# A fused transformer block: another order of filler products, the inverse's rows loaded behind their stores, evictions ahead, and ten operations on another engine

## The chip, the cores and the metric

The kernel runs on one core of a Trainium2 chip. The time is that of the device for one execution, in microseconds; the profile shows one such execution with its five engines: TensorE (PE), VectorE (DVE), ScalarE (ACT), GpSimd (POOL) and the sync engine (SP), which issues the transfers.

## The reference

One transformer block on a sequence of 1024 tokens of width 1024, batch 1, in float32:

```python
mod = silu(c) @ w_ada + b_ada                  # shifts, scales, gates
h = rmsnorm(x) * (1 + sc1) + sh1
q_a, k_a, v_a, q_d, k_d, v_d, z_d, b_d, a_d = split(h @ w_in)
y_attn  = dilated_attention(q_a, k_a, v_a)     # 8 heads of 64, 3 branches
y_delta = gated_deltanet(q_d, k_d, v_d, z_d)   # 8 heads of 64
x = x + g1 * (concat(y_attn, y_delta) @ w_out)
h = rmsnorm(x) * (1 + sc2) + sh2
x = x + g2 * ((silu(h @ w_gate) * (h @ w_up)) @ w_down)   # d_ff 2816
return rmsnorm(x)
```

In the delta part, q, k and v pass a causal convolution of width 4 and a silu. The sequence is cut into chunks of 64. Each chunk and head needs the solution of a unit lower triangular 64x64 system built from k, its decays and beta, and then a scan over the chunks carries a 64x64 state. The output is normalised per head, multiplied by the gain `delta_norm_g` of 64 numbers and by silu(z).

## The kernel before

Every large product is made in three parts, with a high and a low half of both operands (names ending in h and l: `hh`, `hl`, `wh_...`, `wl_...`; the loaded weight is `wr_...`). ScalarE makes the high half, another engine subtracts to get the low half.

**Groups and filler.** The delta heads are worked in two groups of four, `delta(0)` and `delta(1)`. Their chains are long and narrow, so TensorE is given other products between their steps: the generator `others()` yields projections in small pieces, and `turn(...)` emits some of them before each step. The projections are those of the second group (kd, qd, vd by `group1`; each of them is spilled to memory for later), the gates z0 and z1 of both groups (`proj_t` with `z_evac`), and the attention's values va0, va1 and its keys and queries a4_*, a0_* (`proj_d` with `spill`). `until(...)` runs the filler up to a named projection and `hold(what, us)` runs it up to one and then some microseconds more, as the plan counts them; `LEVELS` gives the two arguments for each group. The modulation's later columns (`mods`, from loads `wm` of 512 KB) come in bursts inside the filler, unless `quiet[0]` is set.

**Evictions.** A finished filler product sits in one of two PSUM banks. ScalarE copies it to a buffer of a ring of four (tag `ev`): zt by a Silu (line 634), va (line 1087), sp_* (line 1096). The sync engine stores the buffer. POOL multiplies zt by the gain before the store (line 635).

**The inverse.** `delta_prep` makes lt, the off-diagonal parts, and stores it (line 813). `delta_v` convolves v and multiplies by beta (vd, trv, vb). `delta_inverse` loads lt back as rows (nt, line 870), multiplies them (line 875) and solves 32x32 blocks in 31 pairs of VectorE operations (tm, tt; lines 886 and 890). The result goes to memory and back as tn (lines 893 and 895). Four heads then build the 64x64 and 128x128 inverses: the first product lv (line 918) needs tn, as do ScalarE's copies to `t64`, named tc (lines 924 and 925), and VectorE's transposes to U (line 923). The heads start `SKEW` steps apart, and no modulation is emitted while they run. `delta_scan` follows.

**After the scan** the rest of the filler runs inside the attention, and y is loaded with its halves (`y_load`, line 1403 on), multiplied by w_out and normalised.

**The feed-forward part** uses sums of operands to save products, in two levels. x2[k, half] is the normalised input. At its start, t2[k], T1, T2, T3, T4, H11, H21 and H22 are such sums or single tiles, each split by `h2_split(name, k, tile, engine)`: ScalarE makes the high half (line 1472), the engine named makes the low half by a subtraction (line 1473). `sub` is a difference (line 1596). The products of gate (wga, wgb, wgc) and up (wua, ...) take them in the order H11, H21, then for the last weights T2, T1, T3, H22, T4.

Within an engine the order is that of the priorities that the code gives while it is emitted; an instruction waits for all that stands ahead of it on its engine.

## Time and profile before

| | |
|---|---|
| median of 3 runs | 1410.61 us (1410.28 to 1413.69) |
| the profiled execution | 1409.24 us, its span 1407.2 us |
| mean granted TensorE clock | 0.993 |
| TensorE busy | 1347.5 us, 96% of the span |
| VectorE, ScalarE, POOL busy | 875.2, 661.7, 285.8 us |
| modulation loads (wm) | 44 of 512 KB, 6.2 us to landing |

A row of a timeline is: start in us, duration, engine, line and operation, output <- input, shape, and in brackets the idle time before it with what ended it. A row of the windows gives the stretch, its length, the busy time of PE, PEld, DVE, ACT and POOL with instruction counts, the granted clock, the share of the DMA engines and GB/s. A row of waits gives the total in us, how often, and the longest. A row of grouped instructions gives busy time and the mean in ns. The time outside the span is 2.0 us.

### The profile page before, as it was taken

Reading aid. Unit: us, or ns where it says so; the run is one execution under the profiler, and the core shown is the slowest. Engines: PE = TensorE matmul, PEld = TensorE weight load, DVE = VectorE, ACT = ScalarE, POOL = GpSimd, SP = SyncE. Lnnn points to the kernel's source line nnn. Section 1 sums busy time; section 2 is a strip of 40 time slices with the busy share of each in tenths; the row PEclk is TensorE's granted clock in tenths of the full one; section 3 lists DMA queues with packets and bytes.
Section 4 is the critical chain, followed back from the end, with each engine's and each line's share of the span. In section 5 each row is a group of like instructions: output and inputs, shape, how many; then the busy total and the mean of one; then the engine's idle time right before and its main releaser. Section 6 shows DMA issues by size and latency. Waiting matters only on the chain.

```text
span 1407.2 us, 24465 instructions
## 1 busy us (share of the span) xinstructions
PE 1347.5 (96%) x8984; PEld 1109.5 (79%) x8984; DVE 875.2 (62%) x1669; ACT 661.7 (47%) x1287; POOL 285.8 (20%) x267
## 2 busy tenths in 40 slices
PE   8999999998989899999989999999999999999997
PEld 4778877888878677777877878888888888888885
DVE  3687484656815533666227986667585776474487
ACT  4497514356224355766147743333333333444456
POOL 2345412444303344453153000000000000000000
PEclk9999999999999999999999999999999999999999
DMA  8665575486352345621485345545363665765566
GB/s 307 224 194 167 153 214 164 134 255 186 109 143 65 125 138 145 195 97 61 160 247 175 130 158 171 173 148 174 131 206 105 213 211 185 253 224 194 195 225 232
DMA packets 169872, 245.68 MB, mean 175 GB/s; under 512 B 32566, under 2 KB 73831, under 8 KB 169752
## 3 DMA queue, kind: packets, MB, share of 16 engines
q1 hardware_dynamic: 169752, 244.12, 53.5%
q8 instruction: 71, 1.16, 0.3%
q14 instruction: 49, 0.40, 0.1%
HBM read 181.30 MB, written 67.48 MB: 177 GB/s over the span
## 4 chain that ended last, share of the span: by engine, by line
PE 58%; DVE 3%; DMA 2%; issue 1%; ACT 1%; POOL 0%; SPq 0%; DVEq 0%; ACTq 0%; POOLq 0%
PE wua L1590 8%; PE wga L1590 8%; PE X L1785 6%; PE wo L590 5%; PE wgc L1590 4%; PE wuc L1590 4%; PE Z L1785 4%; PE g_a L590 3%; PE y L1348 3%; PE wgb L1590 2%; PE Y L1785 2%; PE wub L1590 2%; PE tr L1331 2%; PE S L1307 1%; PE S L1308 1%
## 5 line engine op out<-in xcount | busy, mean ns | idle before, releaser
L1580 DVE TENSOR_TENSOR wl_db<-wr_db,wh_db 128x512 fp32r<-128x512 f32 x77 | 53.2, 691 | 76.2 <-ACT wh_db L1579 75.9
L1579 ACT CAST wh_db<-wr_db 128x512 fp32r<-128x512 f32 x77 | 47.9, 622 | 98.4 <-PE X L1785 41.3
L1311 DVE CUSTOM_DVE_ANT_0 X<-S,ng 128x512 f32<-128x512 f32 (+3 forms) x64 | 36.9, 586 | 56.2 <-PE S L1308 37.8
L1785 PE MATMUL X<-wl_db,wh_da 128*128 128x512 f32 x176 | 68.6, 390 | 0.2 <-DVE wl_db L1580 0.2
L1785 PE MATMUL X<-wh_db,wh_da 128*128 128x512 f32 x176 | 68.6, 390 | 0.0
L1785 PE MATMUL X<-wh_db,wl_da 128*128 128x512 f32 x176 | 68.5, 389 | 0.0
L1316 ACT ACTIVATE X<-X,sc 128x128 f32<-128x128 f32 (+7 forms) x64 | 49.4, 773 | 38.3 <-DVE sc L1311 34.8
L1318 POOL TENSOR_SCALAR X<-X,sc 128x128 f32<-128x128 f32 (+7 forms) x64 | 50.5, 792 | 75.9 <-DVE sc L1317 72.6
L1580 DVE TENSOR_TENSOR wl_da<-wr_da,wh_da 128x512 fp32r<-128x512 f32 x77 | 52.7, 685 | 1.2 <-ACT wh_da L1579 1.2
L590 PE MATMUL g_a<-hh,wh_a 128*128 128x512 f32 x128 | 52.8, 412 | 0.0
L590 PE MATMUL wo<-yh,wh_wo 128*128 128x512 f32 x128 | 51.3, 403 | 0.8 <-DVE xo L1399 0.8
L590 PE MATMUL wo<-yl,wh_wo 128*128 128x512 f32 x128 | 50.4, 393 | 1.1 <-DVE yl L1410 1.1
L590 PE MATMUL g_a<-hh,wl_a 128*128 128x512 f32 x128 | 51.2, 400 | 0.0
L590 PE MATMUL g_a<-hl,wh_a 128*128 128x512 f32 x128 | 51.1, 399 | 0.0
L590 PE MATMUL wo<-yh,wl_wo 128*128 128x512 f32 x128 | 51.0, 398 | 0.0
L1579 ACT CAST wh_da<-wr_da 128x512 fp32r<-128x512 f32 x77 | 47.3, 616 | 5.9 <-PE wua L1590 5.8
L1331 PE MATMUL tr<-ident,X 128*128 128x128 f32 x288 | 44.0, 277 | 3.6 <-DVE et L1334 2.0
L1579 ACT CAST wh_wg_s<-wg_s 128x512 fp32r<-128x512 f32 x33 | 20.6, 623 | 56.1 <-PE wuc L1590 23.8
L231 POOL TENSOR_TENSOR wl_wo<-wr_wo,wh_wo 128x512 fp32r<-128x512 f32 x24 | 32.9, 1374 | 61.6 <-ACT wh_wo L230 61.6
L613 PE MATMUL g_va<-wh_va,hh 128*128 128x256 f32 x128 | 38.6, 301 | 5.8 <-ACT sp_a L1096 5.8
L1331 PEld LDWEIGHTS tr<-ident,X 128*128 128x128 f32 x288 | 33.2, 140 | 13.3 <-issue 4.3
L1348 PE MATMUL y<-et,va 128*64 128x128 f32 x576 | 43.2, 280 | 0.3 <-DVE yl L1360 0.3
(544 smaller groups left out, 4304.3 us busy)
## 6 DMA issues: line engine op xcount, KB each, us to landing
wm<-in_wada SPq DMA_DIRECT2D x44, 512.0 KB, 6.2
wr_da<-ao_d SPq DMA_DIRECT2D x77, 256.0 KB, 3.0
wr_wu<-in_wu SPq DMA_DIRECT2D x50, 256.0 KB, 2.8
wr_wg<-in_wg SPq DMA_DIRECT2D x48, 256.0 KB, 2.8
ao_d<-a SPq DMA_DIRECT2D x44, 256.0 KB, 2.3
wr_wd<-in_wdn SPq DMA_DIRECT2D x44, 256.0 KB, 3.0
wr_db<-wt_d SPq DMA_DIRECT2D x44, 256.0 KB, 2.8
ao_d<-as SPq DMA_DIRECT2D x33, 256.0 KB, 2.0
```

The source lines that it names most:

```text
L231: (eng or nc.gpsimd).tensor_tensor(out=lo[:, :n], in0=raw[:, :n], in1=hi[:, :n].bitcast(F32), op=ALU.subtract)
L590: last[0] = nc.tensor.matmul(ps, a[:, w0], b[k0 + k4][:, cs], start=(i == 0), stop=(i == n - 1))
L613: last[0] = nc.tensor.matmul(ps[:, :n], a[k][:, ts_], b[:, w0], start=(i == 0), stop=(i == 23))
L1311: nc.vector.tensor_tensor_reduce(out=X[:, c0:c1], in0=ps[:, 0 : c1 - c0], in1=ng[:, u + c0 : u + c1], scale=1.0, scalar=(3e38 if m is None ...
L1316: nc.scalar.activation(X[:, 0:nk], X[:, 0:nk], AF.Exp, scale=-1.0, bias=m, accum_out=sc[:, 2:3])
L1318: nc.gpsimd.tensor_scalar(out=X[:, 0:nk], in0=X[:, 0:nk], scalar1=sc[:, 3:4], scalar2=0.0, op0=ALU.mult, op1=ALU.add)
L1331: nc.tensor.transpose(ps[:, (kb - c0) * P : (kb - c0 + 1) * P], X[:, kb * P : kb * P + P], ident)
L1348: nc.tensor.matmul(yps[64 * e : 64 * e + 64, yc], va[:, kb, 64 * e : 64 * e + 64], ets[e][:, kb, :], start=(kb == 0), stop=(kb == qb),)
L1579: nc.scalar.copy(hi, src)
L1580: (eng or nc.vector).tensor_tensor(out=lo, in0=src, in1=hi.bitcast(F32), op=ALU.subtract)
L1590: nc.tensor.matmul(ps, a[:, w0], b, start=(first and k == 0 and n_ == 0), stop=(k == 3 and n_ == 2), skip_group_check=True,)
L1785: nc.tensor.matmul(bank[b], a[:, ts_], w, start=(first and f == 0 and n_ == 0), stop=(f == NF - 1 and n_ == 2), skip_group_check=True,)
```

## The change

1. The filler's order. Before: z0, then kd, qd, vd of the second group, z1, then va0, a4_0, a0_0, va1 and so on. After: kd, qd, z0, vd, va0, z1, a4_0, a0_0, va1 and so on. `LEVELS` names z0 instead of qd for the first group's heads, and 24 us instead of 46 for the second's; the first group's scan waits for z0 instead of qd.
2. nt and bpr are loaded by a new `delta_rows_in`, right behind the stores of lt and ahead of `delta_v`. From the second group's last v on, eviction stores and modulation loads are emitted behind that load (`held`), and no modulation is emitted from there to the end of the heads. The modulation's products are tied behind the last filler product emitted.
3. ScalarE's copies tc from tn are tied behind the last eviction emitted before the heads (`evicted`).
4. The gain leaves zt and is applied where y is loaded, as a column of 128 numbers (`ngc`): a multiplying ScalarE copy and a scalar_tensor_tensor on VectorE.
5. In the feed-forward part, the low halves of H22 (four), the differences x2[4+k, 0] - t2[k] (four) and the low halves of T4 for k = 0 and 1 move from VectorE to POOL.

```diff
 EARLY = 1
-LEVELS = ("qd", 4), ("z1", 46)
+LEVELS = ("z0", 4), ("z1", 24)
 TAIL = 4
...
     dtb = small("dtb", [P, 8], I["dtb"].to_broadcast([P, 8]))
-    ngh = small("ngh", [P, 64], I["ng"].to_broadcast([P, 64]))
+    ngc = small("ngc", [P, 1], I["ng"])
 
...
     kd, qd = {}, {}
-    last = [None]
+    last, taken = [None], [None]
     fill = [None]
...
             with urgent():
-                nc.scalar.activation(zt, ps[:, 0:256], AF.Silu)
-            nc.gpsimd.tensor_tensor(
-                out=zt.rearrange("p (h d) -> p h d", h=4),
-                in0=zt.rearrange("p (h d) -> p h d", h=4),
-                in1=ngh.unsqueeze(1).to_broadcast([P, 4, 64]), op=ALU.mult,
-            )
-            nc.sync.dma_start(_.zg[TB * g + tb], zt)
+                taken[0] = nc.scalar.activation(zt, ps[:, 0:256], AF.Silu)
+            with held():
+                nc.sync.dma_start(_.zg[TB * g + tb], zt)
         return f
...
 
-    def delta_v(g, st, vps):
+    gate = [None]
+
+    def held():
+
+        return tc.issue_after(gate[0].ins) if gate[0] else ExitStack()
+
+    def delta_rows_in(g, st):
+
+        nt = pr.tile([P, 32, 32], F32, name=f"nt{g}", tag="dt", bufs=2)
+        rows = nc.sync.dma_start(nt.rearrange("p j i -> p (j i)"), _.lt[g])
+        bpr = pd.tile([P, 32], F32, name=f"bpr{g}", tag="nbpT", bufs=1)
+        nc.sync.dma_start(
+            bpr, bass.AP(tensor=_.bp[g].tensor, offset=_.bp[g][0:1, :].offset, ap=[[32, P], [1, 32]])
+        )
+        st["nt"] = nt, bpr
+        return rows
+
+    def delta_v(g, st, vps, rows):
         st["vb"] = []
...
             conv(8 + hp, vps[q](), vd)
+            if g == q == 1:
+                gate[0], quiet[0] = rows, True
             vb = pd.tile([P, 8, P], F32, name=f"vb{hp}", tag="vb", bufs=2)
...
 
-        nt = pr.tile([P, 32, 32], F32, name=f"nt{g}", tag="dt", bufs=2)
-        nc.sync.dma_start(nt.rearrange("p j i -> p (j i)"), _.lt[g])
-        bpr = pd.tile([P, 32], F32, name=f"bpr{g}", tag="nbpT", bufs=1)
-        nc.sync.dma_start(
-            bpr, bass.AP(tensor=_.bp[g].tensor, offset=_.bp[g][0:1, :].offset, ap=[[32, P], [1, 32]])
-        )
+        nt, bpr = st["nt"]
         nc.vector.tensor_tensor(
...
                 nc.vector.transpose(U[bs, :, bs], tnh[bs])
-            nc.scalar.copy(t64[0:32, :, 0:32], tnh[0:32])
-            nc.scalar.copy(t64[32:64, :, 32:64], tnh[32:64])
+            with tc.issue_after(evicted.ins):
+                nc.scalar.copy(t64[0:32, :, 0:32], tnh[0:32])
+                nc.scalar.copy(t64[32:64, :, 32:64], tnh[32:64])
             yield
...
                     hold(*LEVELS[g])
-                    front, quiet[0] = last[0].ins, True
+                    front, evicted, quiet[0] = last[0].ins, taken[0], True
                 heads.append(head(step // SKEW))
...
             with urgent():
-                nc.scalar.copy(t, ps[:, 0:256])
-            nc.sync.dma_start(_.va[c][:, :, tb].rearrange("i p d -> p i d"), t.rearrange("p (i d) -> p i d", i=2))
+                taken[0] = nc.scalar.copy(t, ps[:, 0:256])
+            with held():
+                nc.sync.dma_start(_.va[c][:, :, tb].rearrange("i p d -> p i d"), t.rearrange("p (i d) -> p i d", i=2))
         return f
...
                 with urgent():
-                    nc.scalar.copy(t, ps[:, 256 * i : 256 * i + 256])
-                nc.sync.dma_start(dst[:, HALF * hf + 256 * i : HALF * hf + 256 * i + 256], t)
+                    taken[0] = nc.scalar.copy(t, ps[:, 256 * i : 256 * i + 256])
+                with held():
+                    nc.sync.dma_start(dst[:, HALF * hf + 256 * i : HALF * hf + 256 * i + 256], t)
         return f
...
                 t0 = 16 + 4 * i
-                with urgent(), tc.issue_after(last[0].ins if i + k0 > 0 else loads[0].ins):
+                with urgent(), tc.issue_after(last[0].ins if i + k0 > 0 else loads[0].ins), held():
                     nc.sync.dma_start(
...
             for k, w in enumerate(ws_, k0):
-                rows4(ps, cc[:, k : k + 32], w, 4, k == KT - 1, k == 0)
+                with tc.issue_after(last[0].ins) if last[0] else ExitStack():
+                    rows4(ps, cc[:, k : k + 32], w, 4, k == KT - 1, k == 0)
             ws_ = after
...
 
+        yield from group1(("kd", "qd"))
         yield from proj_t(I["wz0"], 256, "z0", z_evac(0))
-        yield from group1(("kd", "qd", "vd"))
-        yield from proj_t(I["wz1"], 256, "z1", z_evac(1))
-        done.add("z1")
+        done.add("z0")
+        yield from group1(("vd",))
         for hp in range(4):
...
                 done.add(f"va{hp}")
+            if hp == 0:
+                yield from proj_t(I["wz1"], 256, "z1", z_evac(1))
+                done.add("z1")
             for col, kk in ((KA, 4), (QA, 0)):
...
         delta_prep(g, st, norms[g], kt[0:2], delta_rows(g))
+        rows = delta_rows_in(g, st)
         if g == 1:
             until(lambda: "vd" in done)
-        delta_v(g, st, [lambda q=q: vxp[q] if g == 0 else fetch(4 + q, f"v{2 + q}") for q in range(2)])
+        delta_v(g, st, [lambda q=q: vxp[q] if g == 0 else fetch(4 + q, f"v{2 + q}") for q in range(2)], rows)
         delta_inverse(g, st)
-        until(lambda: ("qd", "z1")[g] in done)
+        until(lambda: ("z0", "z1")[g] in done)
         delta_scan(g, st)
...
 
-    def y_load(k, src):
+    def y_load(k, src, gain=None):
         for hf in range(2):
...
             nc.sync.dma_start(r, src[:, cs])
-            nc.scalar.copy(yh[k][:, cs], r)
-            nc.vector.tensor_tensor(out=yl[k][:, cs], in0=r, in1=yh[k][:, cs].bitcast(F32), op=ALU.subtract)
+            if gain is None:
+                nc.scalar.copy(yh[k][:, cs], r)
+                nc.vector.tensor_tensor(out=yl[k][:, cs], in0=r, in1=yh[k][:, cs].bitcast(F32), op=ALU.subtract)
+            else:
+                nc.scalar.mul(yh[k][:, cs], r, gain)
+                nc.vector.scalar_tensor_tensor(
+                    out=yl[k][:, cs], in0=r, scalar=gain, in1=yh[k][:, cs].bitcast(F32), op0=ALU.mult, op1=ALU.subtract
+                )
 
...
         for k in range(4, 8):
-            y_load(k, _.yd[k // 2 - 2][k % 2])
+            y_load(k, _.yd[k // 2 - 2][k % 2], ngc)
         fill[0] = out_delta()
...
     for k in range(4):
-        h2_split("H22", k, x2[4 + k, 1], nc.vector)
+        h2_split("H22", k, x2[4 + k, 1], nc.gpsimd)
     for k in range(4):
-        sub(x2[4 + k, 0], x2[4 + k, 0], t2[k])
-        h2_split("T4", k, x2[4 + k, 0], nc.vector)
+        sub(x2[4 + k, 0], x2[4 + k, 0], t2[k], nc.gpsimd)
+        h2_split("T4", k, x2[4 + k, 0], nc.gpsimd if k < 2 else nc.vector)
     sx.close()
...
         "dtb": ct(A["dt_bias"]),
-        "ng": ct(A["delta_norm_g"]),
+        "ng": ct(np.tile(A["delta_norm_g"].reshape(64), 2).reshape(P, 1)),
         "wfirst": ct(first.reshape(KT, P, 512)),
```

The sync queue around the load of the second group's rows, before (nt1 and bpr1 are the rows, lt1_d their stored parts, zt and va eviction buffers, wm modulation loads):

```order
L813 DMA lt1_d_1094<-dt1_3_3559 32x8x32
L1119 DMA wm_7_0_4376<-in_wada 128x2x512
L1119 DMA wm_7_2_4378<-in_wada 128x2x512
L813 DMA lt1_d_1094<-dt1_3_3559 32x8x32 x3
L640 DMA zg15_d_1089<-zt1_7_4055 128x256
L1088 DMA va0_d_1072<-va0_0_4108 128x2x128
L1088 DMA va0_d_1072<-va0_1_4137 128x2x128
L1088 DMA va0_d_1072<-va0_2_4186 128x2x128
L870 DMA nt1_4226<-lt1_d_1094 128x1024
L872 DMA bpr1_4228<-bp1_d_1092 128x32
```

and after:

```order
L229 DMA wr_a0_0_0_4488<-in_wd 128x512
L229 DMA wr_a0_0_1_4494<-in_wd 128x512
L809 DMA lt1_d_1094<-dt1_2_3546 32x8x32 x3
L809 DMA lt1_d_1094<-dt1_3_3551 32x8x32 x4
L850 DMA nt1_3828<-lt1_d_1094 128x1024
L1132 DMA wm_6_4_5075<-in_wada 128x2x512
L1132 DMA wm_6_6_5077<-in_wada 128x2x512
L1100 DMA va0_d_1072<-va0_7_4051 128x2x128
L636 DMA zg8_d_1082<-zt1_0_4104 128x256
L636 DMA zg9_d_1083<-zt1_1_4132 128x256
```

The load nt1 follows the last store of lt1_d directly; zg8 to zg10 and the wm_6 loads stand behind it.

ScalarE around the heads' first copies in the second group, before (sp_a0_0_1 and va1_0 are evictions, tc copies from tn1, wh casts of weights):

```order
L1096 COPY sp_a0_0_0_1_4626<-g_a0_0_0_4598 128x256
L230 CAST wh_va1_3_4680<-wr_va1_3_4679 128x512
L924 COPY tc_1_0_4851<-tn1_4328 32x8x32
L925 COPY tc_1_0_4851<-tn1_4328 32x8x32
L230 CAST wh_a4_1_0_5615<-wr_a4_1_0_5614 128x512
L1096 COPY sp_a0_0_1_0_4655<-g_a0_0_1_4629 128x256
L1096 COPY sp_a0_0_1_1_4658<-g_a0_0_1_4629 128x256
L924 COPY tc_1_1_4917<-tn1_4328 32x8x32
L925 COPY tc_1_1_4917<-tn1_4328 32x8x32
L924 COPY tc_1_2_4994<-tn1_4328 32x8x32
L925 COPY tc_1_2_4994<-tn1_4328 32x8x32
```

and after:

```order
L1108 COPY sp_a0_0_0_0_4525<-g_a0_0_0_4500 128x256
L1108 COPY sp_a0_0_0_1_4528<-g_a0_0_0_4500 128x256
L230 CAST wh_va1_3_4581<-wr_va1_3_4580 128x512
L230 CAST wh_a4_1_0_5611<-wr_a4_1_0_5610 128x512
L1108 COPY sp_a0_0_1_0_4556<-g_a0_0_1_4531 128x256
L1108 COPY sp_a0_0_1_1_4559<-g_a0_0_1_4531 128x256
L1098 COPY va1_0_4611<-g_va1_0_4586 128x256
L935 COPY tc_1_0_4631<-tn1_4297 32x8x32
L936 COPY tc_1_0_4631<-tn1_4297 32x8x32
L935 COPY tc_1_1_4697<-tn1_4297 32x8x32
L936 COPY tc_1_1_4697<-tn1_4297 32x8x32
```

Both halves of sp_a0_0_1 and the first va1 stand ahead of tc_1_0 now, and so does the cast of wh_a4_1_0.

VectorE where the feed-forward part's last sums are made, before:

```order
L1473 TENSOR_TENSOR H22l0_8719<-x2_4_1_8147,H22h0_8718 128x512
L1473 TENSOR_TENSOR H22l1_8721<-x2_5_1_8148,H22h1_8720 128x512
L1473 TENSOR_TENSOR T3l3_8749<-x2_3_1_8146,T3h3_8748 128x512
L1473 TENSOR_TENSOR H22l2_8723<-x2_6_1_8149,H22h2_8722 128x512
L1473 TENSOR_TENSOR H22l3_8725<-x2_7_1_8150,H22h3_8724 128x512
L1596 TENSOR_TENSOR x2_4_0_8151<-x2_4_0_8151,t2_0_9039 128x512
L1596 TENSOR_TENSOR x2_5_0_8152<-x2_5_0_8152,t2_1_9048 128x512
L1596 TENSOR_TENSOR x2_6_0_8153<-x2_6_0_8153,t2_2_9057 128x512
L1473 TENSOR_TENSOR T4l0_8751<-x2_4_0_8151,T4h0_8750 128x512
L1599 TENSOR_TENSOR wg0_u5_9149<-wga0_8758,wg0_u5_9149 128x512
L1473 TENSOR_TENSOR T4l1_8753<-x2_5_0_8152,T4h1_8752 128x512
L1473 TENSOR_TENSOR T4l2_8755<-x2_6_0_8153,T4h2_8754 128x512
```

after:

```order
L1497 TENSOR_TENSOR T3l2_8731<-x2_2_1_8129,T3h2_8730 128x512
L1620 TENSOR_TENSOR x2_3_1_8130<-x2_7_1_8134,x2_3_1_8130 128x512
L1497 TENSOR_TENSOR T4l2_8739<-x2_6_0_8137,T4h2_8738 128x512
L1497 TENSOR_TENSOR T4l3_8741<-x2_7_0_8138,T4h3_8740 128x512
L1497 TENSOR_TENSOR T3l3_8733<-x2_3_1_8130,T3h3_8732 128x512
L1708 TENSOR_TENSOR a11_0_9191<-p1_wg0_8756,p1_wu0_8822 128x512
```

and on POOL after, at the end of its program, where nothing stood before:

```order
L1620 TENSOR_TENSOR x2_4_0_8135<-x2_4_0_8135,t2_0_9023 128x512
L1620 TENSOR_TENSOR x2_5_0_8136<-x2_5_0_8136,t2_1_9032 128x512
L1620 TENSOR_TENSOR x2_6_0_8137<-x2_6_0_8137,t2_2_9041 128x512
L1497 TENSOR_TENSOR H22l0_8703<-x2_4_1_8131,H22h0_8702 128x512
L1497 TENSOR_TENSOR H22l1_8705<-x2_5_1_8132,H22h1_8704 128x512
L1497 TENSOR_TENSOR H22l2_8707<-x2_6_1_8133,H22h2_8706 128x512
L1497 TENSOR_TENSOR H22l3_8709<-x2_7_1_8134,H22h3_8708 128x512
L1620 TENSOR_TENSOR x2_7_0_8138<-x2_7_0_8138,t2_3_9050 128x512
L1497 TENSOR_TENSOR T4l0_8735<-x2_4_0_8135,T4h0_8734 128x512
L1497 TENSOR_TENSOR T4l1_8737<-x2_5_0_8136,T4h1_8736 128x512
```

Ten operations have moved; T4l2, T4l3 stay on VectorE, now ahead of T3l3, and read what POOL writes.

## The prediction

> **What bounds the kernel now.** I read the page first (busy time, chain), then the waits of TensorE, then the windows to place them, then the engines' timelines around the longest one.
>
> ```profile
> PE 1347.5 (96%) x8984; PEld 1109.5 (79%) x8984; DVE 875.2 (62%) x1669; ACT 661.7 (47%) x1287; POOL 285.8 (20%) x267
> PE 58%; DVE 3%; DMA 2%; issue 1%; ACT 1%; POOL 0%; SPq 0%; DVEq 0%; ACTq 0%; POOLq 0%
> ...
> PE g_va L613 <- ACT sp_a L1096: 5.8, 1, 5.8
> PE trv L857 <- ACT vd L557: 4.5, 3, 2.4
> PE wua L1590 <- ACT wh_wu_s L1579: 1.2, 1, 1.2
> ```
>
> TensorE is busy 1347.5 of 1407.2 us and carries the chain. The change takes no product away and adds none, so it can only move the 60 us in which TensorE is idle, or that lie in a lower clock. The first wait line is the largest that touches the edited code.
>
> ```profile
> 389.02 0.28 PE L613 MATMUL g_va<-wl_va,hh 128*128 128x256 f32 x1
> 395.06 0.58 PE L613 MATMUL g_va<-wh_va,hh 128*128 128x256 f32 x1 [5.77 <-ACT sp_a L1096]
> 395.44 0.41 PE L613 MATMUL g_va<-wh_va,hl 128*128 128x256 f32 x1
> ...
> 400.78 0.29 PE L613 MATMUL g_va<-wl_va,hh 128*128 128x256 f32 x1
> 400.90 0.28 PE L613 MATMUL g_va<-wh_va,hh 128*128 128x256 f32 x1
> ...
> 390.00:400.00 10.00, 4.94 (x23) 4.94 (x24) 1.74 (x4) 3.84 (x10) 1.27 (x1) 0.70 0.79 206
> ```
>
> The matmul at 400.78 is the 27th after the one at 389.02. At the step of 0.12 us between the last two rows of matmuls it would have started at 389.02 + 27 x 0.12 = 392.26. It is 8.5 us late: 5.8 us of waiting, the rest because the granted clock falls (0.70 over the window) and a matmul takes 0.41 instead of 0.28 us.
>
> **Why it waits.** ScalarE stands in front of a copy of tn, the inverse's rows, which is not there yet. The evictions sp_a that would free a PSUM bank stand behind it in ScalarE's order.
>
> ```profile
> 393.00 0.40 ACT L924 COPY tc<-tn 32x256 f32<-32x256 f32 x1 [8.82 <-DMA tn<-tn_d]
> 394.37 0.64 ACT L1096 COPY sp_a<-g_a 128x256 f32<-128x256 f32 x2
> ...
> 385.85 0.32 SPq L893 DMA_DIRECT2D tn_d<-tt  x1
> 388.53 0.37 SPq L895 DMA_DIRECT2D tn<-tn_d  x1
> ...
> 351.82 0.69 DVE L860 TENSOR_TENSOR vb<-trv,beta 128x512 f32<-128x512 f32 x1 [1.90 <-PE trv L857]
> 353.03 1.22 DVE L875 TENSOR_TENSOR nt<-nt,bpr 128x1024 f32<-128x1024 f32 x1
> 355.15 0.31 DVE L218 STREAM_TRANSPOSE t<-tri 128x128 f32<-128x128 f32 x1 [0.91 <-ACT tri L1137]
> 355.38 0.15 DVE L886 TENSOR_TENSOR tm<-nt,tt 128x31 f32<-128x31 f32 x1
> 385.63 0.19 DVE L890 TENSOR_TENSOR tt<-tt,tm 128x31 f32<-128x31 f32 x1
> 393.08 1.79 DVE L923 STREAM_TRANSPOSE U<-tn 32x256 f32<-32x256 f32 x4 [7.25 <-DMA tn<-tn_d]
> ...
> 412.16 1.20 PE L918 MATMUL lv<-tn,dt 32*32 32x32 f32 x64
> ```
>
> So tn's path is VectorE's 30 us of tm and tt steps, then 7.2 us from the end of the last one to the landing (385.82 to 393.00). TensorE reaches lv, the first product that needs tn, at 412.16, long after tn. What hurts is the ScalarE order, not tn itself.
>
> **The change, part by part.**
>
> *Evictions ahead of the copies.* The hole as it stands goes: -8.5 us.
>
> *Fewer products ahead of lv.* In the new order 231 instead of 336 va matmuls stand ahead of the first lv, and the four bursts of the modulation that stood there are behind it. At 0.12 us, and at 1.08 us for a burst (below), that is 12.6 + 4.3 us. They are not saved, they come behind. But TensorE now reaches lv at 412.16 - 8.5 - 12.6 - 4.3 = 386.8, and tn must be there.
>
> ```profile
> 353.70 1.08 PE L211 MATMUL mods<-wm,cc 128*32 128x128 f32 x32
> ...
> 342.87 3.74 SPq L1088 DMA_DIRECT2D va_d<-va  x3
> 346.80 0.34 SPq L870 DMA_DIRECT2D nt<-lt_d  x1
> ...
> 312.68 1.28 ACT L634 ACT_TABLE_LOAD   x1
> 317.05 1.28 ACT L771 ACT_TABLE_LOAD   x1
> 341.23 1.28 ACT L557 ACT_TABLE_LOAD   x1 [2.98 <-DVE vd L553]
> ```
>
> *tn earlier.* The rows' load nt no longer stands behind three stores of va on the sync queue, and the nt multiply moves ahead of the last vb, into the 1.90 us in which VectorE waited there. That is 1.2 us, the 0.9 us wait for tri goes with the modulation, and the two transposes and sums of the modulation inside the chain give about 0.6. tn then lands at 393.0 - 2.7 = 390.3, the late bound. Early bound: the second z's Silu no longer falls among the decays, so the loads at 312.68 and 317.05 go, and the one at 341.23 is done by a z eviction before vd needs it. If all three (3.8 us) are on tn's path, it lands at 386.5. TensorE is there at 386.8, less the 1.3 us of its own table wait below, so it waits between 1.0 and 4.8 us. The second step of the heads needs the U transposes (1.79 us), which before were done long ahead: up to 0.9 us more. With the lost clock, which cost 2.7 us in the old hole, the price is 1 to 8.4. I take 2.5, nearer the low end, since TensorE and tn gain from the same table loads.
>
> *Table loads on the path.* TensorE's 2.4 us wait for vd held one load: -1.3 us, bounds -2.4 (the whole wait) and 0 (it is back as a wait for the conv).
>
> *Held stores and loads.* The stores of four eviction buffers and the loads wm queue behind nt's load; nt's load waits for its own stores. The wm loads of the last modulation come late, and their matmuls stand in TensorE's order inside the heads:
>
> ```profile
> wm<-in_wada SPq DMA_DIRECT2D x44, 512.0 KB, 6.2
> ```
>
> From the order I estimate about 5 us of products (some 40 at 0.12 us) between their issue and their use, so a wait of some 1 us, bounds 0 and 3. I take +0.5, because the fill around it is also what the wait covers.
>
> *Gain folded into y's load.* 16 multiplies less on POOL, and eight scalar_tensor_tensor in place of eight subtractions on VectorE: 0. Cover: TensorE's products of wo, which waited 1.1 us for yl once; without cover, eight times the difference of 0.07 us between the 0.75 and the 0.68 us of such operations in the rows below.
>
> *Ten operations from VectorE to POOL, before the gate and up products of the second half.* This part speaks against the change.
>
> ```profile
> 744.88 1.78 DVE L1473 TENSOR_TENSOR H11l<-x,H11h 128x512 fp32r<-128x512 f32 x1
> 748.29 0.68 DVE L1473 TENSOR_TENSOR H11l<-x,H11h 128x512 fp32r<-128x512 f32 x1
> 748.89 1.41 DVE L1503 SCALAR_TENSOR_TENSOR x<-x,G,rs 128x512 f32<-128x512 f32 x2
> 753.95 3.18 DVE L1503 SCALAR_TENSOR_TENSOR x<-x,G,rs 128x512 f32<-128x512 f32 x2
> 783.18 0.75 DVE L1503 SCALAR_TENSOR_TENSOR x<-x,G,rs 128x512 f32<-128x512 f32 x1
> ...
> 711.36 1.29 POOL L231 TENSOR_TENSOR wl_wo<-wr_wo,wh_wo 128x512 fp32r<-128x512 f32 x1 [1.43 <-ACT wh_wo L230]
> 753.58 3.00 POOL L1541 TENSOR_TENSOR acc<-acc,sq 128x512 f32<-128x512 f32 x2 [5.76 <-ACT sq L1540]
> ...
> 805.51 1.89 DVE L1596 TENSOR_TENSOR x<-x,t 128x512 f32<-128x512 f32 x3
> 814.46 0.50 PE L1590 MATMUL wua<-T2h,wh_wu_s 128*128 128x512 f32 x1 [1.24 <-ACT wh_wu_s L1579]
> 815.62 0.50 PE L1590 MATMUL wua<-T2h,wl_wu_s 128*128 128x512 f32 x1 [0.42 <-DVE wl_wu_s L1580]
> ...
> 790.00:800.00 10.00, 10.00 (x46) 8.29 (x45) 10.00 (x17) 6.80 (x13) 0.00 (x0) 1.00 0.18 65
> ```
>
> VectorE is fully busy in that stretch (10.00 of 10.00), and TensorE follows it closely: it waits 1.24 and 0.42 us right after. Ten operations at the 0.60 us that three of them take apart (1.89 for three) are 6.0 us less for VectorE. But while POOL works, VectorE's operations with two inputs in SBUF stand still: two of them took 3.18 us beside two on POOL (3.00 us) and 1.41 us without, so each POOL operation cost VectorE 0.9 us. Ten cost 9, and VectorE ends 3 us later than before instead of 6 earlier. Bounds: -1.7 if POOL's work falls into gaps (the two waits go), and 9.0 us less slack at the top, from POOL's own 1.5 us apiece in that row (15.0 - 6.0). Of the 3 us, half is absorbed where products stand ready ahead of need. I take +1.5. Nothing else covers it: without the slack it is 3.
>
> A rule speaks to this. The Trainium skill, "SBUF — State Buffer", section "Who interferes with whom", says that a VectorE instruction with two SBUF inputs contends with a GpSimd one that reads SBUF, and that the port pair is an exclusive lock on which the loser blocks entirely. The rows agree that VectorE is held (3.18 against 1.41 us), by less than POOL's whole duration. By the rule in full, ten times 1.29 us are lost, and this term would be 12.9 - 6.0 = 6.9 instead of 1.5.
>
> *Left over.* The 16.9 us of products that come behind lv go into the scan and the attention stage, where TensorE has short waits; 0, with -1.5 as the best case if they fill some, and +1 if evictions collide there.
>
> **The sum.** -8.5 + 2.5 - 1.3 + 0.5 + 1.5 = -5.3 us. The profiled execution took 1409.24 us (span 1407.2 and 2.0 around it), so it would take 1403.9. The median of the three runs shown, 1410.61, is 1.4 above that execution, so the median after is 1405.3.
>
> **Rivals.** About 0.3%, 4.2 us, is what a measurement of this kernel can tell from no change: faster is below 1406.4, slower above 1414.8.
>
> 1. *The hole closes and POOL hides its work.* lv waits 1.0 at its early bound, POOL falls into gaps (-1.7): -8.5 + 1.0 - 1.3 + 0.5 - 1.7 = -10.0, 1400.6. For it: tn and TensorE arrive within about 1 us of each other by the early bound. Against: VectorE has no gap between 790 and 800.
> 2. *The hole moves to lv.* tn is at its late bound, TensorE waits 5.7 us there and loses 2.4 to the clock, 5.6 more than the sum has: +0.3, 1410.9, no change. For it: tn's path is 30 us of VectorE steps that the change does not shorten. This is also the rival that the change does not do what it says.
> 3. *POOL holds VectorE for its whole length.* Place: the T2, T1, T3, H22 and T4 products at 799 to 813. At 15.0 us for ten, VectorE is 9.0 us late; if the waits of TensorE there are long enough to lower the clock as at 395, 2.7 more. The sum is -5.3 - 1.5 + 11.7 = +4.9, 1415.5, slower. It decides above 11.0 us lost there. For it: VectorE is saturated and two T4 lo operations that stay on it now wait for POOL by way of ScalarE. Against: 0.9 us per operation measured. With 1.29 us apiece, the duration of a POOL operation alone (12.9 - 6.0 = 6.9 us), it is -5.3 - 1.5 + 6.9 = +0.1, 1410.7, no change: that is what the Trainium skill's rule above gives.
>
> **Chances.** The forecast 45%, rival 1 12%, rival 2 18%, rival 3 in the form that ends slower 12%, in its mild form 8%, anything else 5%, split 3 to 2. Part of the forecast's own spread (7 of its 45) lies above 1406.4. That gives faster 0.53, same 0.33, slower 0.14. The range 1398 to 1413 reaches from below rival 1 over rival 2 and the mild rival 3, and leaves out the slower end.
>
> **What would show it.** Right: the wait of g_va for sp_a is gone from TensorE's waits; the granted clock of that stretch is 1.00; lv starts near 388 with a wait of 1 to 3 us; ACT_TABLE_LOAD is two fewer. The VectorE rows between 780 and 815 stretch to 1.4 us or more wherever a POOL row runs, and TensorE's waits at T2, T3 or T4 total 2 to 4 us. Wrong: a wait over 4 us at lv with a low clock (rival 2), T products that wait over 6 us (rival 3), or a wait for zt or sp_a evictions behind the held stores, which none of the terms holds at more than 0.5.

## The result, and the profile after

| | before | after |
|---|---|---|
| median | 1410.72 us (20 runs, 1405.68 to 1415.06) | 1405.52 us (20 runs, 1400.93 to 1411.42) |
| ratio of the two | | 0.9966, interval 0.9955 to 0.9978 |
| the profiled execution, its span | 1409.24, 1407.2 us | 1407.41, 1405.6 us |
| mean granted TensorE clock | 0.993 | 0.991 |

The forecast was 1405.3 us, and the kernel took 1405.52. The total came out within 0.3 us although several of its terms were far off. The profiled execution of after lies 1.9 us above its median and that of before 1.5 us below, so the spans differ by 1.6 us where the medians differ by 5.2.

The page of the changed kernel, busy times and chain:

```profile
PE 1353.3 (96%) x8984; PEld 1113.2 (79%) x8984; DVE 874.6 (62%) x1659; ACT 660.0 (47%) x1285; POOL 287.2 (20%) x261
PE 71%; DVE 13%; DMA 6%; ACT 4%; issue 3%; POOL 1%; SPq 0%; DVEq 0%; ACTq 0%; POOLq 0%
```

TensorE has as many instructions as before (8984) and is busy 5.8 us longer: some matmuls became slower. The waits of TensorE in the changed kernel:

```profile
PE g_z L613 <- POOL wl_z L231: 3.1, 1, 3.1
PE wga L1614 <- ACT wg_u L1670: 2.2, 1, 2.2
PE yt L1075 <- DVE o L1065: 2.2, 4, 1.4
...
PE g_z L613 <- ACT zt L634: 1.9, 1, 1.9
...
PE wga L1614 <- DVE T2l L1497: 1.8, 1, 1.8
PE x2t L1476 <- DVE x L1553: 1.6, 2, 1.0
...
PE wua L1614 <- DVE wl_wu_s L1604: 0.9, 1, 0.9
...
PE st L1009 <- DVE R L1000: 0.7, 1, 0.7
...
PE lv L928 <- DMA tn<-tn_d: 0.7, 1, 0.7
...
PE wgc L1614 <- DVE p_wg L1623: 0.5, 1, 0.5
```

The wait of g_va for sp_a is gone, and lv waits only 0.7 us. New are a wait of g_z for a weight's low half (3.1 us) and one for zt (1.9 us). At the start of the feed-forward part the waits (wg_u, T2l, wl_wu_s, p_wg) come to 5.4 us; the kernel before had 1.2 and 0.4 there.

The same profile around lv, the timelines of TensorE and VectorE:

```profile
393.40 1.20 PE L928 MATMUL lv<-tn,dt 32*32 32x32 f32 x64 [0.67 <-DMA tn<-tn_d]
...
355.70 0.18 DVE L896 TENSOR_TENSOR tm<-nt,tt 128x31 f32<-128x31 f32 x1
384.67 0.19 DVE L900 TENSOR_TENSOR tt<-tt,tm 128x31 f32<-128x31 f32 x1
393.45 1.78 DVE L933 STREAM_TRANSPOSE U<-tn 32x256 f32<-32x256 f32 x4 [8.59 <-DMA tn<-tn_d]
```

The chain of tm and tt starts no earlier than before (355.70 against 355.38), ends 1.0 us earlier (384.86 against 385.82), and its way through memory takes 8.6 us instead of 7.2. So tn lands at 393.4, not between 386.5 and 390.3. TensorE, forecast at lv for 386.8, comes there at 392.7, and the two meet.

What made both late stands 55 us earlier in the same profile, in the timelines of POOL, TensorE and ScalarE and in a window:

```profile
332.42 5.74 POOL L836 TENSOR_TENSOR qd<-qd,eb 128x1024 f32<-128x1024 f32 x2 [7.09 <-ACT eb L835]
338.10 2.25 POOL L231 TENSOR_TENSOR wl_z<-wr_z,wh_z 128x512 fp32r<-128x512 f32 x1
...
337.03 0.28 PE L613 MATMUL g_z<-wh_z,hl 128*128 128x256 f32 x1
340.41 0.58 PE L613 MATMUL g_z<-wl_z,hh 128*128 128x256 f32 x1 [3.10 <-POOL wl_z L231]
340.79 0.41 PE L613 MATMUL g_z<-wh_z,hh 128*128 128x256 f32 x1
...
346.34 1.04 PE L872 MATMUL trv<-ident,vd 128*128 128x128 f32 x8
...
341.95 1.05 ACT L557 ACTIVATE vd<-vd 128x1024 f32<-128x1024 f32 x1
...
340.00:350.00 10.00, 9.59 (x60) 9.59 (x61) 4.02 (x5) 2.86 (x4) 3.63 (x4) 0.70 0.37 92
```

The transposes trv in the kernel before:

```profile
343.64 1.09 PE L857 MATMUL trv<-ident,vd 128*128 128x128 f32 x8 [2.36 <-ACT vd L557]
```

The new order of the filler puts z1 where va0's products ran before. The low half of its last slab stands on POOL behind the two long multiplications of qd, and TensorE waits 3.1 us for it. The granted clock then falls to 0.70 for the ten microseconds from 340, in which a matmul takes 0.41 instead of 0.28 us. The transposes trv stand behind these products in TensorE's order. Their input, the Silu of vd, is done at 343.0, but they start at 346.34, without a wait of their own; before, they started at 343.64, as soon as the Silu was done. So vb and then the chain of tm and tt come later than the prediction had them.

**Where the time went, by stages.** Four points in each trace: the end of the last kk_k (the second group's products before the inverse), the start of the first lv of the second group, the start of the x2t product that waits for xt (the last transposes before the feed-forward part), and the end. Times in us of one execution each, so that differences of a few tenths mean nothing:

| | to kk_k | kk_k to lv | lv to x2t | x2t to the end | TensorE idle, lv to x2t |
|---|---|---|---|---|---|
| before | 334.0 | 78.1 | 340.8 | 654.2 | 19.0 |
| after | 333.4 | 60.0 | 349.2 | 663.0 | 10.6 |

By the prediction's count, 16.9 us of products went behind lv, and TensorE's busy time in the stage lv to x2t grew by as much (321.85 to 338.63 us, first row before, second after):

```profile
412.16:752.96 340.80, 321.85 (x2469) 259.68 (x2468) 171.23 (x470) 173.16 (x377) 138.02 (x133) 1.00 0.43 133
393.40:742.64 349.24, 338.63 (x2701) 278.05 (x2701) 170.87 (x478) 178.58 (x390) 136.92 (x133) 1.00 0.48 146
```

The stage grew by only 8.4 us: its idle time fell by 8.4. Before, these waits stood there (1.9 of the 3.2 us of yt lie in the first group's scan, outside this stage):

```profile
PE yt L1064 <- DVE o L1054: 3.2, 7, 1.2
...
PE x2t L1452 <- DVE x L1529: 2.7, 2, 1.6
PE tr L1331 <- DVE et L1334: 2.0, 3, 0.7
PE st L998 <- DVE R L989: 1.9, 1, 1.9
...
PE S L1307 <- DVE sc L1311: 1.6, 3, 1.2
```

After, yt has no wait left in this stage, x2t and st wait 1.6 and 0.7 us, and tr and S wait 0.7 us each for et and sc. Two traces do not say which part of the change did that; the amount of filler is tried below.

The last stage grew by 8.8 us. There are two causes. One is the ten operations on POOL; the timelines of POOL, VectorE and TensorE in the changed kernel, and the clock:

```profile
778.49 4.78 POOL L1497 TENSOR_TENSOR H22l<-x,H22h 128x512 fp32r<-128x512 f32 x3 [2.76 <-ACT H22h L1496]
...
780.32 1.79 DVE L1497 TENSOR_TENSOR T2l<-t,T2h 128x512 fp32r<-128x512 f32 x1
792.35 0.68 DVE L1497 TENSOR_TENSOR T2l<-t,T2h 128x512 fp32r<-128x512 f32 x1
...
793.09 0.50 PE L1614 MATMUL wga<-T2l,wh_wg_s 128*128 128x512 f32 x1 [1.75 <-DVE T2l L1497]
799.55 0.50 PE L1614 MATMUL wga<-T3h,wh_wg_s 128*128 128x512 f32 x1 [2.24 <-ACT wg_u L1670]
...
800.00:810.00 10.00, 10.00 (x38) 7.70 (x36) 7.34 (x13) 3.41 (x6) 0.00 (x0) 0.83 0.70 235
```

An operation of VectorE takes 1.79 us beside one of POOL and 0.68 us otherwise. The other cause was not foreseen. The matmuls that use the tiles H11 and H21 became slower, all through the part; durations as smallest, median and largest in ns, first before, then after:

```profile
L1590 PE MATMUL wua<-H11h,wh_wu x44: 389/389/475, 772.1 to 1170.9; 128*128 128x512 f32 x44
```

```profile
L1614 PE MATMUL wua<-H11h,wh_wu x44: 393/396/477, 760.8 to 1169.4; 128*128 128x512 f32 x44
```

There are 528 products with H11h, H11l, H21h and H21l. Their step, from the start of one to the start of the next, grows from 227.5 to 233.8 ns on average in the traces, which is 528 x 6.3 ns = 3.3 us.

### The profile page after: what moved, and what is told of

Its sections match the earlier page's. It is cut to its first block, busy times and chain, and to the rows that moved or that the text cites. A ratio compares the mean times of both kernels' runs of the same rounds, so it can differ in the third digit from the quotient of the medians.

```text
span 1405.6 us, 24430 instructions
## 1 busy us (share of the span) xinstructions
PE 1353.3 (96%) x8984; PEld 1113.2 (79%) x8984; DVE 874.6 (62%) x1659; ACT 660.0 (47%) x1285; POOL 287.2 (20%) x261
## 4 chain that ended last, share of the span: by engine, by line
PE 71%; DVE 13%; DMA 6%; ACT 4%; issue 3%; POOL 1%; SPq 0%; DVEq 0%; ACTq 0%; POOLq 0%
PE wua L1614 8%; PE wga L1614 8%; PE X L1809 6%; PE g_a L590 4%; PE wuc L1614 4%; PE Z L1809 4%; PE wgc L1614 4%; PE wo L590 3%; PE y L1366 2%; PE Y L1809 2%; PE tr L1349 2%; PE g_va L613 2%; DVE tm L896 2%; PE f L251 2%; PE wgb L1614 2%
## 5 line engine op out<-in xcount | busy, mean ns | idle before, releaser
L1603 ACT CAST wh_wg<-wr_wg 128x512 fp32r<-128x512 f32 x31 | 19.3, 621 | 47.2 <-PE wua L1614 19.2
L1603 ACT CAST wh_wu_s<-wu_s 128x512 fp32r<-128x512 f32 x33 | 20.4, 622 | 44.5 <-PE wga L1614 17.5
```

What stands on the lines that cost most here:

```text
L1603: nc.scalar.copy(hi, src)
```

## The experiments

The medians of the kernel before beside these variants were 1410.53, 1410.30 and 1411.23 us; where a variant is set against after, their medians are compared, although the two did not run side by side. The ratios and their intervals are against the kernel before.

### The ten operations back on VectorE (after, one part undone)

```diff
-        h2_split("H22", k, x2[4 + k, 1], nc.gpsimd)
+        h2_split("H22", k, x2[4 + k, 1], nc.vector)
...
-        sub(x2[4 + k, 0], x2[4 + k, 0], t2[k], nc.gpsimd)
-        h2_split("T4", k, x2[4 + k, 0], nc.gpsimd if k < 2 else nc.vector)
+        sub(x2[4 + k, 0], x2[4 + k, 0], t2[k])
+        h2_split("T4", k, x2[4 + k, 0], nc.vector)
```

> The changed kernel with the ten feed-forward operations back on VectorE, nothing else. Theory A (POOL holds VectorE): up to the start of the feed-forward products the changed kernel was 10.3 us ahead in its profile and only 4.7 us ahead at the second T2 product of up, so undoing this part gives 5 to 6 us: about 1400. TensorE's waits for T2l (1.75) and for the copy wg_u (2.24) go, the granted clock at 800 to 810 is 1.00, and the two waits at wua (1.24 and 0.42) come back. Rival (POOL takes work off VectorE at no price, the loss lies elsewhere): 1405.5 or up to 2 us more.

Measured: 1400.44 us against 1410.53 of the kernel before, ratio 0.9928 (0.9900 to 0.9955). That is 5.1 us less than after's median. TensorE's waits in this stretch and the clock:

```profile
800.83 0.50 PE L1614 MATMUL wua<-T2h,wh_wu_s 128*128 128x512 f32 x1 [1.25 <-ACT wh_wu_s L1603]
801.99 0.50 PE L1614 MATMUL wua<-T2h,wl_wu_s 128*128 128x512 f32 x1 [0.42 <-DVE wl_wu_s L1604]
...
800.00:810.00 10.00, 8.74 (x37) 6.96 (x38) 9.96 (x18) 5.25 (x11) 0.00 (x0) 1.00 0.52 171
```

The waits are those of the kernel before, 1.67 us instead of the 5.4 us of after, and the clock stays at 1.00 where after had 0.83 over ten microseconds. 3.7 us of waits and 1.7 us of clock make 5.4, which agrees with the 5.1.

### The ten operations on POOL alone (before, one part done)

The same edit the other way round, on the kernel before.

> The kernel before with only the ten feed-forward operations on POOL. Theory A (VectorE stands while POOL works): 5 us slower, 1415.7, with waits for T2l and wg_u of 2 us each and rows of 1.7 us on VectorE beside POOL's. Rival (VectorE is relieved): 1409, the two waits at wua gone.

Measured: 1416.63 us against 1410.30, ratio 1.0039 (1.0022 to 1.0057): 6.3 us slower. The two new waits are there without the rest of the change:

```profile
PE wga L1590 <- ACT wg_u L1646: 2.2, 1, 2.2
PE wga L1590 <- DVE T2l L1473: 2.2, 1, 2.2
```

So this part costs 5 to 6 us wherever it stands. The clock stays at 1.00 from 790 to 830 us in this execution, so the low clock of after is not a fixed part of the price.

### What of POOL's work holds VectorE

These two variants of the changed kernel have the ten operations on VectorE, and work without use on POOL at that place: ten additions of two SBUF tiles, or one addition and 24 memsets of about the same length in all.

```diff
+    lk = px.tile([P, HALF], F32, name="lk", tag="m", bufs=5)
+    for _i in range(10):
+        nc.gpsimd.tensor_tensor(out=lk, in0=t2[0], in1=t2[0], op=ALU.add)
```

```diff
+    lk = px.tile([P, HALF], F32, name="lk", tag="m", bufs=5)
+    nc.gpsimd.tensor_tensor(out=lk, in0=t2[0], in1=t2[0], op=ALU.add)
+    for _i in range(24):
+        nc.gpsimd.memset(lk, 0.0)
```

> The changed kernel with the ten operations back on VectorE, and ten additions of 128x512 on POOL that nobody reads, tied to t2's first tile. Theory A (a two-input operation of VectorE stands while POOL reads SBUF): rows of VectorE stretch from 0.68 to about 1.8 us beside each, 10 us lost, TensorE waits 8 us or more in all at the T products, 1409. Rival (what costs is that T4 waits for POOL's results): no stretched rows and 1400.4.

> The same with one such addition and 24 memsets of 128x512 on POOL, which write SBUF and read nothing, some 12 us in all. Theory A in the narrow form (only POOL's reads hold VectorE): one stretched row, 1401. In the wide form (any use of SBUF by POOL): rows stretch throughout, 1406 or more. Rival: 1400.4.

Measured, one run each: 1407.50 us with the additions, 1399.65 with the memsets. POOL and VectorE, first beside the additions:

```profile
765.77 14.07 POOL L1765 TENSOR_TENSOR lk<-t 128x512 f32<-128x512 f32 x10 [15.26 <-DVE t L1620]
...
767.29 1.52 DVE L1497 TENSOR_TENSOR T2l<-t,T2h 128x512 fp32r<-128x512 f32 x1
768.73 2.97 DVE L1620 TENSOR_TENSOR x<-x,x 128x512 f32<-128x512 f32 x2
```

and beside the memsets:

```profile
766.35 13.98 POOL L1766 MEMSET lk<- 128x512 f32 x24
...
766.77 0.68 DVE L1497 TENSOR_TENSOR T2l<-t,T2h 128x512 fp32r<-128x512 f32 x1
767.37 1.28 DVE L1620 TENSOR_TENSOR x<-x,x 128x512 f32<-128x512 f32 x2
```

With the additions the two engines take turns: one operation of POOL per 1.41 us, and VectorE starts its operations 1.44 us apart (767.29 to 768.73) instead of 0.60 (766.77 to 767.37). An operation of POOL costs VectorE 0.84 us. Memsets of the same total length cost it nothing. That only reads count is what the Trainium skill says ("SBUF — State Buffer", section "Who interferes with whom"): a VectorE instruction with two SBUF inputs contends with a GpSimd one that reads SBUF and not with one that only writes. That the loser blocks for the whole instruction these rows do not quite show: 0.84 us are lost per operation, and the one addition ahead of the memsets took 1.04.

Nobody reads the additions, and yet TensorE waits 5.1 us in all at the products of gate and up, where it waits 1.6 beside the memsets. That is less than the 8 us expected, but it speaks against the rival, by which the loss comes from T4 waiting for POOL's results.

### The one-column constant

`ngh` had 64 columns and `ngc` has one. Every tile allocated after it lies 252 bytes lower. This kernel gives `ngc` its old room back:

```diff
-    ngc = small("ngc", [P, 1], I["ng"])
+    ngct = const([P, 64], "ngc")
+    ngc = ngct[:, 0:1]
+    nc.sync.dma_start(ngc, I["ng"])
```

> The changed kernel with the gain column in a constant tile of 64 columns (one used), so that what is allocated behind it lies where it lay before. Theory A (the place of tiles in SBUF sets the step of matmuls): the H11 and H21 products take 396 ns in the changed kernel and 389 before, 528 of them with a step 0.006 us longer, 3.1 us; with the padding they take 389 again and the time is about 1402.4. Rival (that profiled execution had a slower step by chance): 1405.5, and H11's duration does not follow the padding.

Measured: 1401.64 us, ratio 0.9926 (0.9901 to 0.9951), 3.9 us less than after's median. The durations are those of the kernel before again:

```profile
L1616 PE MATMUL wua<-H11h,wh_wu x44: 389/389/475, 760.4 to 1164.4; 128*128 128x512 f32 x44
```

The stage from x2t to the end takes 659.7 us instead of 663.0. And the other way round, an unused column of 4 bytes put into the kernel before:

```diff
+    gap = const([P, 1], "gap")
+    nc.vector.memset(gap, 0.0)
```

> The kernel before with a constant of one column allocated behind the gain, so that all that is allocated later lies four bytes further on. Theory A (the place in SBUF modulo some small power of two sets the step): the change moved them by 252 bytes less, the same modulo 256, so the H11 and H21 products take 396 ns and the time is 3 us longer, 1413.8. Rival (it is the distance between two tiles, or a place modulo something larger): 389 ns and 1410.7.

Measured: 1418.60 us (5 runs, 1416.13 to 1424.17) against 1410.30, ratio 1.0060 (1.0034 to 1.0085). The durations rise as in after:

```profile
L1592 PE MATMUL wua<-H11h,wh_wu x44: 393/396/477, 777.2 to 1179.9; 128*128 128x512 f32 x44
```

The last stage takes 658.5 instead of 654.2 us. So the shift causes the longer matmuls, by both tests. The other half of the 8.3 us was not expected. It lies ahead of x2t, in a wait of trv of 4.1 us instead of at most 2.4, the sp_a hole at 6.5 us instead of 5.8, and more low clock; why a shift should do that stays open.

### The evictions ahead of the copies, alone and undone

On the kernel before, only the copies tc are tied behind the last eviction:

```diff
-            nc.scalar.copy(t64[0:32, :, 0:32], tnh[0:32])
-            nc.scalar.copy(t64[32:64, :, 32:64], tnh[32:64])
+            with tc.issue_after(evicted.ins):
+                nc.scalar.copy(t64[0:32, :, 0:32], tnh[0:32])
+                nc.scalar.copy(t64[32:64, :, 32:64], tnh[32:64])
```

> The kernel before with one part of the change: ScalarE's copies from tn tied behind the last eviction. Theory A (ScalarE's order makes the hole): TensorE's wait of 5.77 us for sp_a and the low clock behind it go, TensorE reaches lv 8.5 us earlier, tn long there: about 1402. Rival (the wait reappears in the scan, where less work is left): lv is earlier but the scan's waits grow, and no more than 3 us are gained: 1408.

Measured: 1404.66 us against 1410.30, ratio 0.9957 (0.9941 to 0.9972): 5.6 us faster, on its own as much as the whole change. TensorE and ScalarE in place of the 5.8 us hole, and the window:

```profile
393.82 0.39 PE L613 MATMUL g_va<-wh_va,hh 128*128 128x256 f32 x1 [1.42 <-ACT va L1088]
...
393.40 0.65 ACT L1088 COPY va<-g_va 128x256 f32<-128x256 f32 x2 [4.18 <-DMA qk_d<-sp_a]
...
390.00:400.00 10.00, 8.58 (x72) 8.38 (x71) 1.74 (x4) 1.10 (x4) 0.00 (x0) 1.00 0.91 237
```

The clock stays at 1.00 where it was 0.70. A wait of 1.4 us for another eviction is left, since that one waits for its buffer's store (the row of ScalarE). The time lies between the two expectations; the rival's reason is not seen, since the stage lv to x2t takes 341.7 us where before took 340.8. The reverse, the changed kernel without the tie:

```diff
-            with tc.issue_after(evicted.ins):
-                nc.scalar.copy(t64[0:32, :, 0:32], tnh[0:32])
-                nc.scalar.copy(t64[32:64, :, 32:64], tnh[32:64])
+            nc.scalar.copy(t64[0:32, :, 0:32], tnh[0:32])
+            nc.scalar.copy(t64[32:64, :, 32:64], tnh[32:64])
```

> The changed kernel without that part: ScalarE's copies from tn stand ahead of the sp_a evictions again. Theory A: TensorE stops at the second va bank at about 391, until tn has landed (393.4), the copies and a cast are done and sp_a is evicted (about 397): 6 us of waiting and up to 2.5 for the clock, less the 1.5 us that lv waits now: 1410 to 1412. Rival (the earlier load of the rows alone closes the hole): 1405.5.

Measured: 1426.69 us (4 runs, 1414.23 to 1435.37), ratio 1.0106 (1.0039 to 1.0173), some 21 us above after's median, several times what was expected. The hole is back at its old size:

```profile
395.95 0.58 PE L613 MATMUL g_va<-wh_va,hh 128*128 128x256 f32 x1 [6.54 <-ACT sp_a L1107]
...
400.00:450.00 50.00, 50.00 (x633) 42.29 (x627) 14.51 (x38) 9.66 (x26) 4.12 (x6) 0.50 0.29 78
```

But in this execution (1435.37 us, the longest of the four) the clock stays at 0.50 for the fifty microseconds behind it, with TensorE busy throughout. Half the clock for 50 us is up to 25 us of work. The runs differ by 21 us among themselves. Only one was profiled, but the mean granted clock was measured in each: 0.971, 0.973, 0.981 and 0.988, from the longest run to the shortest. The difference of 0.017 over some 1420 us is 24 us, so the low clock accounts for the spread. The shortest run, 1414.23 us, is 8.7 us above after's median, near what was expected; why the clock stayed low for so long in the others is open.

### The new hole at z1

The low half of z1's last slab is made on VectorE instead of POOL:

```diff
-        slabs = list(slabs) + [wsplit(src[s], 2 * n, f"{name}_{s}") for s in range(len(slabs), 4)]
+        slabs = list(slabs) + [
+            wsplit(src[s], 2 * n, f"{name}_{s}", nc.vector if (name, s) == ("z1", 3) else None) for s in range(len(slabs), 4)
+        ]
```

> The changed kernel with one subtraction moved: the low half of the second z's last weight slab is made by VectorE instead of POOL, where it stands behind two multiplications of q by its decays. Theory A: TensorE's wait of 3.10 us for wl_z and the 2.4 us lost to the clock behind it go; tn comes some 3.5 us earlier, since ScalarE's vd stood behind the z eviction, and lv waits 2 us more, so 3 to 4 us in all: 1402. Rival (tn is the limit in this stage): lv waits 5 us more and the time stays at 1405.5.

Measured: 1406.55 us (12 runs, 1401.62 to 1421.14), ratio 0.9964 (0.9937 to 0.9990): no gain over after. The hole itself did shrink, and the matmul behind it takes 0.39 instead of 0.58 us:

```profile
335.10 0.39 PE L615 MATMUL g_z<-wl_z,hh 128*128 128x256 f32 x1 [1.43 <-DVE wl_z L231]
```

lv starts at 386.96 instead of 393.40, but 3.6 of these 6.4 us were there already at the end of kk_k, ahead of the edit. The waiting x2t product comes at 741.33 instead of 742.64, so 1.3 us are left. The stage lv to x2t takes 354.4 us where after took 349.2, and TensorE's idle time from 200 us behind lv to x2t is 9.4 instead of 6.1 us. In five variants of the changed kernel (this one, the memsets, the room for `ngc`, the ten operations back, and all repairs together), lv starts between 386.96 and 390.17 and x2t between 739.57 and 741.42. It seems that something other than TensorE's products sets the time of x2t once lv is early enough; what, was not settled.

### The amount of filler ahead of lv

The changed kernel with the old amount of filler after z1, 22 us more ahead of lv as the plan counts:

```diff
-LEVELS = ("z0", 4), ("z1", 24)
+LEVELS = ("z0", 4), ("z1", 46)
```

> The changed kernel with 46 instead of 24 us of filler ahead of the second group's heads: by the order 153 va and 27 more a4 matmuls, some 24 us, stand ahead of lv instead of behind it. Theory A (filler left for the scan and the attention fills their waits): the 450 to 500 stretch loses 6 us of busy TensorE again, and the time is 5 to 7 us longer, 1411.5; lv waits 0 instead of 0.7. Rival (what is left over changes nothing): 1405.5, or 1404 by the lv wait.

Measured: 1407.78 us against 1411.23, ratio 0.9969 (0.9948 to 0.9991), 2.3 us above after's median. From 450 to 500 TensorE is busy 46.38 instead of 49.15 us, 2.8 less where 6 were expected. The first lv comes at 414.39, 21 us later than in after, and the stage from it to x2t:

```profile
414.39:742.22 327.83, 314.27 (x2522) 252.17 (x2521) 171.54 (x474) 172.32 (x377) 133.23 (x129) 1.00 0.49 147
```

TensorE has 24.4 us less to do here than in after (314.27 against 338.63) and even 7.6 less than before. Its idle time is 13.6 us. In the four kernels that have the change's code up to x2t (after, the ten operations back, the additions and the memsets) it is 10.2 to 11.9, and before had 19.0. The direction is that of filler covering waits: yt waits 2.7 us in this stage, where after has no wait of yt. But it is 1.7 to 3.4 us, and x2t comes at 742.22, where after has it at 742.64. The other 5.4 us by which the idle time fell do not come from the amount of filler. In this run as in after, the waits of wo for yl and of S for yt (1.1 us each before) are gone, and those for et, R and sc are shorter (0.8, 0.7 and 0.4 us). Which part of the change does that was not tested.

### All three repairs together

The ten operations on VectorE, the room for `ngc`, and z1's slab on VectorE.

> All three edits together. Theory A, with the three adding up: 5.5 + 3.1 + 3.5 = 12.1 us below the changed kernel, about 1393.5. Rival (they share one cover, VectorE's order): no better than the best of the three alone, about 1400.

Measured: 1396.58 us (1392.33 to 1404.91) against 1410.53, ratio 0.9895 (0.9860 to 0.9930). It is faster than both kernels: 14 us below before and 8.9 below after. The sum of the first two repairs from after, 5.1 + 3.9 = 9.0, gives 1396.5; by these medians the third added nothing here either. The time lies halfway between the two expectations, 1393.5 with the third repair at 3.5 us and 1400.

## Why the prediction was right, and where its terms were not

The total was right because errors of both signs cancelled, and that is luck. The terms, as the prediction put them, beside what the runs give:

| term | predicted | measured | from |
|---|---|---|---|
| the hole goes | -8.5 | -5.6 | evictions alone, on the kernel before |
| ten operations on POOL | +1.5 | +5.1 (+6.3 on before) | undone on after, done on before |
| placement of the tiles | not seen | +3.9 | undone on after |
| lv, table loads, held loads, left-over filler | +1.7 | -8.6 | what is left of -5.2 |
| sum | -5.3 (1410.6 to 1405.3) | -5.2 | medians |

The last measured entry is a difference, -5.2 + 5.6 - 5.1 - 3.9, and no run isolates it; each variant's interval reaches 2 to 4 us to either side. The traces come near it: x2t comes at 752.96 us before, at 747.21 with the evictions alone, and between 739.57 and 742.64 in the four kernels that have the change's code up to there, so 4.6 to 7.6 us more were gained ahead of x2t.

Of the signs that the prediction named, most came: the wait for sp_a is gone, the clock is 1.00 from 390 to 400, there are two table loads fewer (19 instead of 21), VectorE's operations stretch beside POOL's, and the waits at T2l and T3h sum to 4.0 us. That lv starts near 388 after a wait of 1 to 3 us did not come (393.40 and 0.7).

- **The hole (-8.5).** The mechanism was right: the copies of tn held back the evictions. Sized alone it is worth 5.6 us. The step that failed is that all evictions would then be free: after the tie they wait for stores, 1.4 us in the kernel with the tie alone. The other 1.5 us of the difference are within the interval.
- **lv waits (+2.5, within 1 to 8.4).** It waits 0.7 us, and its second step 0.8 more for VectorE (`cs`). The size was near, the working was not: tn was to land between 386.5 and 390.3 and TensorE to be there at 386.8. Both came 3 to 7 us later. The step that failed is that the earlier load of nt and the table loads put tn 2.7 to 6.5 us earlier. What it names did happen (nt is multiplied ahead of the last vb, the wait for tri and the table load in front of vd are gone), but the hole of z1 took it back: trv starts 2.7 us later in TensorE's order (346.34 against 343.64), and the way through memory is 1.4 us longer. With z1's slab on VectorE, trv starts at 339.79 and the chain at 349.20 instead of 355.70, 3.6 us of it won ahead of kk_k.
- **Table loads (-1.3).** There are two loads fewer on ScalarE. Their gain on the path is not seen on its own: the wait of the second group's trv for vd, 2.4 us before, is gone, but trv stands behind the hole of z1 in its place.
- **Held stores and loads (+0.5).** No wait for wm loads shows in TensorE's rows. The wait of g_z for zt, 1.9 us, stands between 200 and 300 us in z0's products, whose place is new; that is ahead of the held stores, and the prediction did not price it.
- **The new hole at z1.** Not foreseen; the nearest sign was "a wait for zt or sp_a evictions". It was a low half on POOL that TensorE waited for, 3.1 us and 2.5 more of clock (25 steps from 340.41 to 345.91 instead of 0.12 us apiece). Taking most of it away gained nothing in the median, so by the run it is not what the change lost.
- **Ten operations on POOL (+1.5).** The price per operation was right: 0.9 us forecast, 0.84 measured with idle additions, 1.1 in place (1.79 against 0.68). Nine of VectorE's operations are stretched in after, by 9.3 us in all, so it ends 9.3 - 6.0 = 3.3 us late, where 3 were forecast. The step that failed is "half is absorbed where products stand ready": nothing was absorbed, TensorE waited 3.7 us more, and in after the clock fell as well, which cost another 1.7. Rival 3's mild form, 6.9 us, was nearer to the 5.1 to 6.3 measured. It priced a whole operation of POOL each time, as the Trainium skill's rule does; the rows do not bear that out in full (1.1 of 1.29 us in place).
- **Left-over filler (0, within -1.5 and +1).** This group of terms has the largest error. The stage lv to x2t took in 16.9 us of products and grew by 8.4, so 8.5 us were gained in it. The waits of before had that much in them (1.3 + 2.7 + 2.0 + 1.9 + 1.6 = 9.5 us of the five rows shown above), and the prediction did not add them up. The obvious reading, that the additional filler covered them, holds for a part: the run that moved it back ahead of lv lost 2.3 us, and 5.4 us of the gain stayed without it. Their cause is open.
- **The gain folded into y's load (0).** Its time was rightly nothing. Its constant was not: the removed 252 bytes cost 3.9 us.

## What to carry to other kernels

Add up the short waits at the new place of moved products before calling their worth nothing, and then move the products alone: two stage tables suggested 8.5 us here, and the run that undid the move found 2.3. An operation given to GpSimd takes VectorE's time as well, when both read two tiles from SBUF, and where VectorE is full that can show at TensorE in full. When the allocation shifts, even by a small constant, compare the durations of unchanged matmuls before looking for any other cause.

## What the runs showed of the hardware that was not expected

- The same matmul of 128x512 took 389 or 396 ns, by where its tiles lay: 4 bytes more in the kernel before, or 252 bytes fewer in after, made 528 products slower, and 64 columns of room made them fast again.
- The clock after a wait is not the same each time. After the 3.1 us wait for wl_z it was 0.70 from 340 to 350 in after, and that is 0.50 from 340 to 346 and 0.99 from 346 to 350; after the same wait of 3.07 us in the kernel with the ten operations back it stayed at 1.00 there. Waits of 1.8 and 2.2 us were followed by 0.50 from 800 to 803 in after, and two of 2.2 us by 1.00 throughout with the ten operations on POOL alone. After 6.5 us it stayed at 0.50 for fifty microseconds of full work. The Trainium skill, "TensorE: Matmul & The Clock Gate", section "What's actually happening", gives about 3.4 us of busy time until the clock is full again; the fifty microseconds do not agree with that. Its section "Seeing it yourself" does tell of a gate seen stuck for 50 us and more, there at a quarter of the clock and here at half.
- Memsets on POOL left VectorE's operations at 0.68 us; additions of the same total length made them 1.52 (one run each).
